# A decoder layer's second norm: four row tiles turned through VectorE and DRAM, gates reordered, and two buffers and chunk sizes changed

## Chip, cores and metric

The kernel runs on one core of one Trainium2 chip. The metric is the device time of one execution in microseconds (us); lower is better. TensorE is called PE, VectorE DVE, ScalarE ACT, GpSimd POOL and SyncE SP. Each is a queue that executes its instructions in order; DMAs are issued by SP, ACT and POOL.

## What is computed

One decoder layer on 1024 tokens and 16 meta tokens ahead of them (1040 rows), model width 1024, in float32. Two head groups share one input projection: sliding-window attention with sinks, and a gated linear recurrence (RG-LRU) behind a causal convolution. Their outputs are joined, projected, normed and added; then a feed-forward block with a squared ReLU is added in the same way.

```
u  = rmsnorm(h, g_pre_mix);  q, k, v, xr, yr = split(u @ w_in)
attn = sliding_window_attention_with_sinks(q, k, v, sinks)       # window 128
xr = causal_depthwise_conv(xr)
r = sigmoid(xr @ w_a + b_a);  i = sigmoid(xr @ w_x + b_x)        # in blocks of 64
a = exp(-8 r softplus(-lambda));  u = sqrt(1 - a^2) * i * xr
hr[t] = a[t] * hr[t-1] + u[t]
mix = concat(attn, gelu(yr) * hr) @ w_out
h = h + rmsnorm(mix, g_post_mix)
u = rmsnorm(h, g_pre_ffn);  f = square(relu(u @ w_ff1)) @ w_ff2
h = h + rmsnorm(f, g_post_ffn)
```

## The kernel before

**Precision.** Nearly every product is made of three matmuls (mm3, L123): each operand is split into a high part (a cast, usually on ACT, L96) and a low part (the rest, on DVE, L99); high x high, high x low and low x high are added in one bank of PSUM (the accumulator memory that PE writes). So a "split" of a tile costs one pass on ACT and one on DVE.

**Order of the work.** The program is written in one order and then put in order for each engine by a scheduler that plans with estimated costs; pieces can be marked as fill ("deferred", with FILL_LAG), so that PE does them where the main line has nothing ready. `behind(name, ins)` adds an order between two instructions (the scheduler must place the second after the first; no wait of its own at run time). Buffers come from pools by a tag: "raw" has 2 slots, "ws" 5, "a" 16, "b" 17, "c" 8, "d" 4 and "e" 2; PSUM banks carry the tags acc, s, pt and o, two of each. A new tile of a tag waits until the tile that last had its slot is no longer read.

**Stages, by the trace's times.**

1. To about 55 us: first norm, transposes, keys, values and the first queries.
2. To about 192 us: attention in eight steps (`scores`, `attend`, from L610 on), each step one pair of heads and one quarter of the rows. A step ends with a drain: ACT copies half of a bank, DVE adds the other half (L705, L706). Between the steps stand the fills: projections of two query groups, of four chunks of x (`fill_x`) and of four chunks of y (`fill_y`). `project` runs over eight slices of the model width and over the column pieces in a list; x uses ALL (272, 256, 256, 256 columns) and y REAL2 (two of 512). DVE copies each finished y piece out (L751).
3. 194 to 211 us: `gates(c)` for four chunks c of the recurrence (L805): three pieces of columns, two gates s, each on one half of PE's rows, three products: 18 matmuls of 64x348 a chunk into the banks s, pt and o in turn, and a sigmoid on ACT per bank (L824, through the helper at L82). Fill matmuls stand between the gates. The first of the sigmoids is preceded by a load of ACT's function table.
4. To about 260 us: `gather`, `decay` (exp and tanh on ACT), `recur` (square root on ACT; scale, product and scan on DVE: L850 to L852), gelu of y, `rec_out` (product with y and the split, L854), for chunks 0 and 1 and then 2 and 3. The output projection's weights are loaded and split among them (`load_wo`, `split_wo`; kc counts its eight slices). kc 0 to 3 take attention and need no recurrence; kc 4 and 5 need chunks 0 and 1, kc 6 and 7 chunks 2 and 3, by `rec_out`.
5. 226 to 332 us: `out_mm(t)` (L922), the output projection of eight tiles of 128 rows; tiles 0 to 3 first do kc 0 to 3, then 4 and 5, and the rest in the loop at L1113. `out_norm(t)` (L938): two reductions (rs, computed with POOL and DVE), scale by gmix_b (L951), residual (L954), a store of the row tile, and the second norm's scale (L959). `u2_tiles(t)` (L962) turns the normed tile with eight PE transposes (L971) and writes the result, times g_ffn_col, from PSUM into u2f: half by ACT (L982), half by DVE (L976). u2f[0] (tiles 0 to 3) and u2f[1] (tiles 4 to 7) are the halves of the feed-forward block's input.
6. To about 630 us: the first feed-forward product as a block scheme with seven instead of eight products. `operand` splits u2f tiles (b11 and b21 from u2f[0]); `t_sums` and `t_rest` form sums of the halves.
7. To the end (953 us): the second one: `steps` are 7 products (i) by 8 slices (q), 56 steps n = 8 i + q. `fetch_2(n)` loads one or two weight blocks into "raw" and "e" (L1261); for some q the second block is added to the first by a DMA of POOL (L1267). `prep_2(n)` splits the result.

Of the kernel before, what the change touches and what calls it, by code (L numbers as in the profile page):

```python
# [9 lines left out]
F32 = mybir.dt.float32  # L10
F32R = mybir.dt.float32r
AF = mybir.ActivationFunctionType
ALU = mybir.AluOpType
# [3 lines left out]
P = 128  # L17
D = 1024
# [19 lines left out]
def hybrid_layer(  # L38
# [248 lines left out]

    ALL = [(0, 272), (272, 256), (528, 256), (784, 256)]
    REAL2 = [(16, 512), (528, 512)]

# [318 lines left out]
    def scores(jp, quarter):  # L609
# [57 lines left out]
            )  # L667
        return sn

    def attend(jp, quarter, sn):  # L670
        flat = sn.rearrange("p a b c -> p (a b c)")
        pp = []
        for h in range(2):

            ph, pl = (slot("c", [P, 4, 2, P], F32R) for _ in range(2))
            pt = bank("pt")
            for i in range(4):
                nc.tensor.transpose(pt[:, i * P : (i + 1) * P], sn[:, h, i, 0:P], ident)
            pt = pt.rearrange("p (a b) -> p a b", a=4)
            split(ph[:, :, 0], pl[:, :, 0], pt)  # L680
            for p_ in (ph, pl):
                for s, g, op in ((1, 1, ALU.is_ge), (0, -1, ALU.is_gt)):
                    nc.gpsimd.affine_select(  # L683
                        out=p_[:, :, s], in_=f32(p_[:, :, 0]), pattern=[[0, 4], [g, P]],
                        compare_op=op, fill=0.0, base=0, channel_multiplier=-g,
                    )
            pp.append((ph, pl))
        kb0 = 2 * quarter
        for h in range(2):
            po = bank("o")  # L690
            two = po.rearrange("p (j c) -> p j c", j=2)
            for n, (oc, pc, w) in enumerate(((0, 0, P), (0, P, 2 * P), (P, 3 * P, P))):
                kb = kb0 + n
                v = vk[h][:, kb - 1, :] if kb else vm[:, h, :]
                for k, p_ in enumerate(pp[h]):
                    nc.tensor.matmul(  # L696
                        two[:, :, oc : oc + w], v,
                        p_.rearrange("p (j i) s c -> p j (i s c)", j=2)[:, :, pc : pc + w],
                        start=n == 0 and k == 0, stop=n == 2 and k == 1,
                        skip_group_check=True,  # L700
                    )

            r, o = HALF[h], HALF[1 - h]
            whole = flat[r, 0:512]
            nc.scalar.copy(whole, po[o, :])  # L705
            nc.vector.tensor_tensor(whole, po[r, :], whole, op=ALU.add)  # L706
        ah, al = at[quarter // 2][jp]
        c = slice(256 * (quarter % 2), 256 * (quarter % 2) + 256)
        split(
            ah[:, :, c], al[:, :, c],  # L710
            flat[:, 0:512].rearrange("p (j c) -> p j c", j=2),
        )
# [26 lines left out]
    def fill_x(c):  # L739
        def run(w):  # L740
            xr, sink = new_x()
            project(w, ALL, sink)
            conv(c, xr, "b" if c == 3 else "d")
        return run

# [59 lines left out]
    def gates(c):  # L805
        ch, cl = pair("b", [P, TT])
        split(ch, cl, xc[c])


        z = [slot("c", [P, TT]) for _ in range(2)]  # L810
        for t0, n in ((0, 348), (348, 348), (696, 344)):
            acc = []
            for s in range(2):
                flip[0] += 1
                acc.append(bank(("s", "pt", "o")[flip[0] % 3]))
            for k, (a, b) in enumerate(((0, ch), (0, cl), (1, ch))):
                for s in range(2):
                    nc.tensor.matmul(
                        acc[s][:, :n], gw[HALF[s], a, c, :], b[HALF[s], t0 : t0 + n],
                        start=k == 0, stop=k == 2, skip_group_check=True,  # L820
                    )
# [116 lines left out]
    def out_norm(t, po):  # L938
        xr = slot("d", [P, D])
        nc.sync.dma_start(xr, x[t * P : (t + 1) * P, :])  # L940
        h = slot("raw", [P, D])
        ssq = [small.tile([P, 1], F32, name=f"sq{n}", tag=f"sq{n}") for n in range(2)]
        for n in range(2):
            c = slice(512 * n, 512 * n + 512)
            nc.scalar.activation(
                h[:, c], po[n], AF.Square, scale=RMS_SC, accum_out=ssq[n]
            )
        rs = rstd_of(ssq)
        for n in range(2):
            c = slice(512 * n, 512 * n + 512)  # L950
            nc.vector.scalar_tensor_tensor(  # L951
                h[:, c], po[n], rs, gmix_b[:, c], op0=ALU.mult, op1=ALU.mult
            )
        nc.vector.tensor_tensor(h, h, xr, op=ALU.add)  # L954
# [4 lines left out]
        nc.vector.tensor_scalar(xr, h, rs2, None, op0=ALU.mult)  # L959
        return xr  # L960

# [34 lines left out]
    def combine(dst, x0, x1, op):  # L996
        return nc.vector.tensor_tensor(dst, x0, x1, op=op).ins  # L997

    def operand(tiles):
        pairs = []  # L1000
        for t_ in tiles:
            hi, lo = pair("b", [P, 2, 512])
            split(hi, lo, t_)
            pairs.append((hi, lo))
        return pairs

# [132 lines left out]
    def t_sums(c):  # L1139
        for i in range(2):  # L1140
            combine(t3[i][:, :, c], u2f[1][2 + i][:, :, c], u2f[1][i][:, :, c], ALU.subtract)
            combine(t2[i][:, :, c], t3[i][:, :, c], u2f[0][i][:, :, c], ALU.add)
            hi, lo = ot2[i]
            split(hi[:, :, c], lo[:, :, c], t2[i][:, :, c])

# [15 lines left out]
    def t_rest(k):  # L1161
        i = k % 2
        if k < 2:
            behind(mark[0], combine(u2f[1][i], u2f[1][i], u2f[0][i], ALU.subtract))
        elif k < 4:
            behind(mark[0], combine(t2[i], u2f[0][2 + i], t2[i], ALU.subtract))
        else:
            hl = pair("a", [P, 2, 512])
            late = mark[0]
# [340 lines left out]
```

## Time and profile before

| | |
|---|---|
| median of 3 runs | 956.37 us (955.89 to 956.82) |
| the profiled execution's own time | 954.71 us |
| its span in the trace | 953.0 us |
| granted TensorE clock in it | 0.999 |

A line of the profile gives a start or a count, the busy time, the engine, the line of the code (often that of a helper: L96, L98 and L99 are the split, L125, L130 and L131 the three products, L82 every table function of ACT, L997 `combine`), the operation, and "out<-in" by the names of tiles and tags, with partitions x elements and type; "x2" says that two instructions are shown as one. In brackets stands the idle time of the engine ahead of it and what ended that. In the list of waits a row says who waited, for whom, the microseconds in total, how often, and the longest. A DMA's row gives its number, size and the median time from issue to landing.

### The profile page before, as it was taken

How to read it: one execution, taken by the hardware profiler on the slowest of the kernel's cores; microseconds unless marked ns; L12 is line 12 of the kernel's file. 1: busy time of each engine (PE TensorE's matmuls, PEld its weight loads, DVE VectorE, ACT ScalarE, POOL GpSimd, SP SyncE). 2: the span in 40 equal slices, each digit the busy share in tenths (PEclk: the TensorE clock that was granted, in tenths of full speed). 3: DMA queues.
4: the chain of work that ended last, by engine and by line, in shares of the span. 5: the costliest groups of instructions: out<-in, count | busy, mean ns of one | idle time of the engine just before them, and what ended most of it. 6: DMA issues, size and time to landing. Idle time of an engine off the chain costs nothing.

```text
span 953.0 us, 12421 instructions
## 1 busy us (share of the span) xinstructions
PE 941.2 (99%) x4712; PEld 787.1 (83%) x4712; DVE 658.9 (69%) x849; ACT 507.8 (53%) x858; POOL 132.1 (14%) x205
## 2 busy tenths in 40 slices
PE   9999999999999999999999999999999999999997
PEld 8999999877888878888888888888888788888885
DVE  6668788879865887665644465476568576769883
ACT  8546766568645564443655575654433343445441
POOL 4104546410020100010000000001111100001201
PEclk9999999999999999999999999999999999999999
DMA  8220011104225468674422364334778765637934
GB/s 272 56 67 23 24 45 44 46 23 133 86 108 174 142 220 266 199 239 151 163 89 88 111 201 131 101 114 117 175 171 202 180 199 178 198 134 201 241 66 89
DMA packets 88199, 130.21 MB, mean 137 GB/s; under 512 B 13702, under 2 KB 52630, under 8 KB 88140
## 3 DMA queue, kind: packets, MB, share of 16 engines
q1 hardware_dynamic: 78972, 104.44, 34.4%
q0 software_dynamic: 8880, 24.19, 11.9%
q8 instruction: 37, 0.61, 0.3%
q10 hardware_dynamic: 288, 0.79, 0.2%
q14 instruction: 22, 0.18, 0.1%
HBM read 109.93 MB, written 18.87 MB: 135 GB/s over the span
## 4 chain that ended last, share of the span: by engine, by line
PE 91%; DVE 5%; ACT 2%; issue 1%; DMA 0%; DVEq 0%; SPq 0%
PE ps_acc L125 10%; PE ps_acc L131 10%; PE ps_acc L130 10%; PE ps_s L131 6%; PE ps_s L130 6%; PE ps_s L125 6%; PE ps_pt L130 6%; PE ps_pt L131 6%; PE ps_pt L125 6%; PE ps_o L131 5%; PE ps_o L130 5%; PE ps_o L125 5%; ACT c L82 1%; PE ps_o L696 1%; PE ps_acc L282 1%
## 5 line engine op out<-in xcount | busy, mean ns | idle before, releaser
L99 DVE TENSOR_TENSOR ws<-raw,ws 128x1024 fp32r<-128x1024 f32 (+1 forms) x69 | 82.6, 1197 | 71.0 <-ACT ws L96 24.1
L96 ACT CAST ws<-raw 128x1024 fp32r<-128x1024 f32 (+1 forms) x68 | 69.7, 1025 | 92.8 <-PE ps_o L130 25.0
L125 PE MATMUL ps_acc<-a,ws 128*128 128x256 f32 (+2 forms) x272 | 88.6, 326 | 0.7 <-DVE b L479 0.4
L130 PE MATMUL ps_acc<-a,ws 128*128 128x256 f32 (+2 forms) x272 | 87.9, 323 | 0.0
L96 ACT CAST ws<-e 128x1024 fp32r<-128x1024 f32 x41 | 43.0, 1050 | 83.4 <-PE ps_o L130 33.2
L131 PE MATMUL ps_acc<-a,ws 128*128 128x256 f32 (+2 forms) x272 | 87.5, 322 | 0.0
L99 DVE TENSOR_TENSOR b<-b,b 128x1024 fp32r<-128x1024 f32 (+2 forms) x50 | 58.9, 1178 | 24.7 <-PE ps_o L130 19.5
L99 DVE TENSOR_TENSOR ws<-e,ws 128x1024 fp32r<-128x1024 f32 x41 | 50.1, 1222 | 33.4 <-ACT ws L96 20.0
L96 ACT CAST b<-b 128x1024 fp32r<-128x1024 f32 (+2 forms) x49 | 50.0, 1019 | 43.6 <-DVE b L997 38.1
L683 POOL TENSOR_SCALAR_AFFINE_SELECT c<-c 128x512 fp32r<-128x512 f32 x64 | 55.5, 884 | 68.9 <-ACT c L96 54.9
L125 PEld LDWEIGHTS ps_acc<-a,ws 128*128 128x128 f32 x272 | 51.3, 188 | 5.4 <-issue 0.9
L131 PEld LDWEIGHTS ps_acc<-a,ws 128*128 128x128 f32 x272 | 51.2, 188 | 4.0 <-issue 0.2
L130 PEld LDWEIGHTS ps_acc<-a,ws 128*128 128x128 f32 x272 | 51.2, 188 | 3.7 <-issue 0.2
L125 PE MATMUL ps_acc<-ws,b 128*128 128x512 f32 (+1 forms) x120 | 46.4, 388 | 1.1 <-ACT ws L96 1.1
L130 PE MATMUL ps_acc<-ws,b 128*128 128x512 f32 (+1 forms) x120 | 46.2, 385 | 0.1
L131 PE MATMUL ps_acc<-ws,b 128*128 128x512 f32 (+1 forms) x120 | 46.2, 385 | 0.0
L125 PE MATMUL ps_pt<-ws,b 128*128 128x512 f32 x112 | 44.2, 395 | 0.0
L131 PE MATMUL ps_pt<-ws,b 128*128 128x512 f32 x112 | 44.1, 394 | 0.0
L130 PE MATMUL ps_pt<-ws,b 128*128 128x512 f32 x112 | 44.1, 393 | 0.0
L125 PE MATMUL ps_s<-ws,b 128*128 128x512 f32 x110 | 43.5, 395 | 0.0
L130 PE MATMUL ps_s<-ws,b 128*128 128x512 f32 x110 | 43.4, 394 | 0.0
L131 PE MATMUL ps_s<-ws,b 128*128 128x512 f32 x110 | 43.2, 393 | 0.0
(413 smaller groups left out, 2660.0 us busy)
## 6 DMA issues: line engine op xcount, KB each, us to landing
raw<-in_w_ff_dram SPq DMA_DIRECT2D x61, 512.0 KB, 3.5
e<-in_w_ff_dram SPq DMA_DIRECT2D x45, 512.0 KB, 4.0
a<-in_w_ff_dram SPq DMA_DIRECT2D x12, 512.0 KB, 5.5
s_dram<-a POOLq DMA_DIRECT2D x12, 512.0 KB, 3.8
raw<-in_w_in_dram SPq DMA_DIRECT2D x9, 512.0 KB, 3.8
c<-in_x_dram SPq DMA_DIRECT2D x8, 512.0 KB, 4.9
d<-in_x_dram SPq DMA_DIRECT2D x8, 512.0 KB, 4.6
out_dram<-raw SPq DMA_DIRECT2D x8, 512.0 KB
```

Of the source, the lines that this page charges most:

```text
L82: ins = nc.scalar.activation(*args, **kwargs).ins
L96: nc.scalar.copy(hi, src)
L99: low = nc.vector.tensor_tensor(lo, src, f32(hi), op=ALU.subtract).ins
L125: ins = nc.tensor.matmul(dst, lh, rh, start=start, stop=False, skip_group_check=True).ins
L130: nc.tensor.matmul(dst, lh, rl, start=False, stop=False, skip_group_check=True)
L131: last_mm[0] = nc.tensor.matmul(dst, ll, rh, start=False, stop=stop, skip_group_check=True).ins.name
L282: last_mm[0] = nc.tensor.matmul(acc[:, :n], w[k // 2][:, kc, :], u[kc][k % 2][:, t0 : t0 + n], start=k == 0 and kc == 0, stop=k == last an ...
L683: nc.gpsimd.affine_select(out=p_[:, :, s], in_=f32(p_[:, :, 0]), pattern=[[0, 4], [g, P]], compare_op=op, fill=0.0, base=0, channel_multip ...
L696: nc.tensor.matmul(two[:, :, oc : oc + w], v, p_.rearrange("p (j i) s c -> p j (i s c)", j=2)[:, :, pc : pc + w], start=n == 0 and k == 0, ...
```

## The change

Five edits in one diff.

- The list THIRDS replaces ALL for x (three pieces of 348, 348 and 344 columns instead of four) and names the gates' pieces, which were the same.
- `attend` remembers its last drain; the first product of both gates of chunk 0's first piece is ordered behind it.
- Tiles 0 to 3 of the second norm no longer go through `u2_tiles`. `u2_store` scales the row tile by rs and by the whole row of g_pre_ffn (a new broadcast tile in a slot of "ws") into an order in which a transpose of 32x32 blocks on DVE gives the wanted layout up to a regrouping of partitions; the result goes to DRAM from a tile of tag "e". `u2_read`, one tile later in the program, brings it back with four DMAs into u2f[0], which now has the shape 128 x 16 x 2 x 32. The sums and splits that read u2f[0] address it in runs of 32.
- The tiles that are still turned on PE come two tiles later in the loop over t: 4 and 5 ahead of the norm of tiles 6 and 7, 6 and 7 behind.
- `fetch_2` takes the second weight block of the products i = 1 and 2 from tag "d" instead of "raw" or "e".

```diff
+    THIRDS = [(0, 348), (348, 348), (696, 344)]
...
-            nc.vector.tensor_tensor(whole, po[r, :], whole, op=ALU.add)
+            drained[0] = nc.vector.tensor_tensor(
+                whole, po[r, :], whole, op=ALU.add
+            ).ins.name
...
-            project(w, ALL, sink)
+            project(w, THIRDS, sink)
...
+                    if c == 0 and t0 == 0 and k == 0:
+                        behind(drained[0], ins)
...
-    u2f = [[None] * 4 for _ in range(2)]
+    u2f = [[slot("c", [P, 16, 2, 32]) for _ in range(4)], [None] * 4]
+    u2_dram = dpool.tile([4, 4, P, 2 * P], F32, name="u2_dram")
+    gpre_b = slot("ws", [P, D])
+    nc.scalar.dma_start(gpre_b, g_pre_ffn[0].partition_broadcast(P))
+
+    def dealt(t_):
+        return t_.rearrange("p (k d b) -> p k d b", k=KC, b=4)
+
+    def u2_store(t, h, rs, tmp):
+        nc.vector.scalar_tensor_tensor(
+            tmp.rearrange("p (b k d) -> p k d b", b=4, k=KC), dealt(h), rs,
+            dealt(gpre_b), op0=ALU.mult, op1=ALU.mult,
+        )
+        y = slot("e", [P, D])
+        nc.vector.transpose(y, tmp)
+        nc.sync.dma_start(u2_dram[t].rearrange("a (d b) r -> (a d) (b r)", b=4), y)
+
+    def u2_read(t):
+        for q in range(4):
+            nc.sync.dma_start(
+                u2f[0][q][:, 4 * t : 4 * t + 4].rearrange("p a k t -> p a (k t)"),
+                u2_dram[t, :, :, 64 * q : 64 * q + 64].rearrange("a p r -> p a r"),
+            )
...
         rs2 = rstd_of([ssq2])
+        if t < 4:
+            u2_store(t, h, rs2, xr)
+            return None
         nc.vector.tensor_scalar(xr, h, rs2, None, op0=ALU.mult)
...
+    def rows(t_, c=slice(0, 512)):
+        if len(t_.shape) == 4:
+            return t_[:, c.start // 32 : c.stop // 32]
+        return t_[:, :, c].rearrange("p k (g t) -> p g k t", t=32)
...
-        for t_ in {4: (0,), 5: (2,), 6: (4,), 7: (5,)}.get(t, ()):
-            u2_tiles(t_, xns[t_])
+        if t > 5:
+            u2_tiles(t - 2, xns[t - 2])
         xns[t] = out_norm(t, po)
-        for t_ in {4: (1,), 5: (3,), 7: (6,)}.get(t, ()):
-            u2_tiles(t_, xns[t_])
+        if 1 <= t <= 4:
+            u2_read(t - 1)
+        if t == 7:
+            u2_tiles(6, xns[6])
...
         tags = (("raw", "e"), ("e", "raw"))[n % 2] if i < 6 else LASTW[q]
+        if i in (1, 2):
+            tags = tags[0], "d"
```

More of the change, by code (lines that the diff above doesn't have):

```diff
@@ L668, in scores @@
         return sn
+    drained = [None]
     def attend(jp, quarter, sn):
@@ L810, in gates @@
         z = [slot("c", [P, TT]) for _ in range(2)]
-        for t0, n in ((0, 348), (348, 348), (696, 344)):
+        for t0, n in THIRDS:
             acc = []
@@ L817, in gates @@
                 for s in range(2):
-                    nc.tensor.matmul(
+                    ins = nc.tensor.matmul(
                         acc[s][:, :n], gw[HALF[s], a, c, :], b[HALF[s], t0 : t0 + n],
                         start=k == 0, stop=k == 2, skip_group_check=True,
-                    )
+                    ).ins
+                    if c == 0 and t0 == 0 and k == 0:
+                        behind(drained[0], ins)
             for s in range(2):
@@ L1002, in operand @@
             hi, lo = pair("b", [P, 2, 512])
-            split(hi, lo, t_)
+            if len(t_.shape) == 4:
+                split(rows(hi), rows(lo), t_)
+            else:
+                split(hi, lo, t_)
             pairs.append((hi, lo))
@@ L1141, in t_sums @@
             combine(t3[i][:, :, c], u2f[1][2 + i][:, :, c], u2f[1][i][:, :, c], ALU.subtract)
-            combine(t2[i][:, :, c], t3[i][:, :, c], u2f[0][i][:, :, c], ALU.add)
+            combine(rows(t2[i], c), rows(t3[i], c), rows(u2f[0][i], c), ALU.add)
             hi, lo = ot2[i]
@@ L1163, in t_rest @@
         if k < 2:
-            behind(mark[0], combine(u2f[1][i], u2f[1][i], u2f[0][i], ALU.subtract))
+            behind(mark[0], combine(rows(u2f[1][i]), rows(u2f[1][i]), u2f[0][i], ALU.subtract))
         elif k < 4:
-            behind(mark[0], combine(t2[i], u2f[0][2 + i], t2[i], ALU.subtract))
+            behind(mark[0], combine(rows(t2[i]), u2f[0][2 + i], rows(t2[i]), ALU.subtract))
         else:
```

## The prediction

> **What bounds the kernel now.** I read the busy shares first, then the list of TensorE's own waits, then ten-microsecond windows.
>
> ```profile
> span 953.0 us, 12421 instructions
> PE 941.2 (99%) x4712; PEld 787.1 (83%) x4712; DVE 658.9 (69%) x849; ACT 507.8 (53%) x858; POOL 132.1 (14%) x205
> ```
> ```profile
> PE ps_acc L308 <- DVE base_e L562: 1.5, 1, 1.5
> PE ps_acc L125 <- ACT ws L96: 1.1, 1, 1.1
> ...
> PE ps_pt L130 <- DVE a L99: 0.2, 1, 0.2
> ```
>
> PE works for 99% of the span, and its seven waits (the first two and the last shown) add up to 4.6 us. So the time is PE's instructions plus those few waits: an edit gains only by taking matmuls off PE or by ending one of the waits, and loses only by making PE wait. Work moved to VectorE (DVE), ScalarE (ACT) or a queue costs nothing until PE runs out of work. The profiled execution's own time is 954.71 us (953.0 span and 1.7 around it). That is 1.66 below the median of 956.37. I sum against 954.71 and add the 1.66 at the end.
>
> **Step 1: tiles 0 to 3 are no longer turned on PE (a gain).**
>
> ```profile
> 281.10 1.03 PE L971 MATMUL ps_o<-ident,d 128*128 128x128 f32 x8
> 281.89 0.48 PE L125 MATMUL ps_acc<-ws,b 128*128 128x512 f32 x1
> 282.21 0.39 PE L130 MATMUL ps_acc<-ws,b 128*128 128x512 f32 x1
> ```
>
> From 281.10 to 282.21 PE spends 1.11 us on eight transposes and one matmul. A matmul alone takes 0.23 (step 2), so a tile's transposes cost 0.88. Four tiles: **-3.5 us**, as PE has no wait there.
>
> In exchange each of the four tiles gets, on DVE, a scaled copy that writes its row in another order, and a transpose of 32x32 blocks, in place of one multiply (L959). SP gets one 512 KB store and four reads of 128 KB in 256-byte runs.
>
> ```profile
> 263.48 1.41 DVE L951 SCALAR_TENSOR_TENSOR raw<-ps_pt,rs,e 128x512 f32<-128x512 f32 x2 [0.75 <-POOL rs L176]
> 264.93 1.23 DVE L954 TENSOR_TENSOR raw<-raw,d 128x1024 f32<-128x1024 f32 x1
> ...
> 268.34 0.75 DVE L959 TENSOR_SCALAR d<-raw,rs 128x1024 f32<-128x1024 f32 x1 [2.12 <-POOL rs L176]
> ```
> ```profile
> 248.99 4.53 DVE L852 TENSOR_TENSOR_SCAN c<-b,b 128x1040 f32<-128x1040 f32 x2
> ```
> ```profile
> s_dram<-a POOLq DMA_DIRECT2D x12, 512.0 KB, 3.8
> ...
> e<-s_dram SPq DMA_DIRECT2D x8, 512.0 KB, 3.2
> ```
>
> No row has either new operation. Lower ends: 0.75 for the transpose (L959), 1.23 for the copy (L954). Upper end for each: the scan, the slowest row per element, at 2.3. I take 1.25 for both, by L954, a plain pass over a tile of the same size. PE hands tiles 0 to 3 over within 11 us (12 matmuls each are left) and then takes 11 for every later tile (48 matmuls), so DVE works off a backlog, and the point to watch is tile 5, whose first matmul (281.89, before the transposes went 281.1) needs tile 2's banks. In the changed order DVE does, from 268.34: copy of tile 0, L951 of tile 1, transpose of tile 0, L954, the wait of 2.12, copy of tile 1, L951 of tile 2: 268.34 + 1.25 + 1.41 + 1.25 + 1.23 + 2.12 + 1.25 + 1.41 = 278.3. Cover 2.8; PE doesn't wait. At 2.3 for each new pass it would be 281.4, a wait of 0.3. Tiles 6 and 7 come 11 and 22 us later and DVE catches up. Then the turned rows: two more such rounds of 7.3 put the end of tile 3's transpose near 294; its store lands near 298 (3.8), the reads near 302 (3.2 by the row, more for the short runs), and the splits (passes of 1.2 like L954) end by 305 for b11 and 308 for b21. PE first multiplies b11 after tile 7, three tiles of 11 behind 281, near 314. Nine us of cover; cost 0.
>
> [...]
>
> **Step 2: x in three pieces (a small gain).**
>
> ```profile
> 72.38 0.28 PE L130 MATMUL ps_acc<-a,ws 128*128 128x256 f32 x1
> ...
> 76.04 0.28 PE L131 MATMUL ps_acc<-a,ws 128*128 128x256 f32 x1
> ```
> ```profile
> 258.87 0.39 PE L125 MATMUL ps_pt<-a,b 128*128 128x512 f32 x1
> ...
> 261.65 0.39 PE L125 MATMUL ps_o<-a,b 128*128 128x512 f32 x1
> ```
>
> Over 31 steps a 256-column matmul takes 3.66 / 31 = 0.118; over 12 steps one of 512 takes 2.78 / 12 = 0.232. Twice 0.118 less 0.232 is 0.004: the fixed part of a matmul. Four chunks x 8 slices x 3 products x 1 piece = 96 matmuls fewer at the same columns: **-0.4**. ACT's four evictions fewer lie beside PE. The scheduler orders the whole attention stage anew, where the list of waits shows under 1 us to win or lose by name; I take 0, within -1 to +2.
>
> **Step 3: the first gates held behind the last attention drain (a loss).** No wait is added, only an order. In the order of the changed kernel, PE does 4 fill matmuls after the last value product, then all gates of chunk 0, then at once those of chunk 1; before, fills stood between.
>
> ```profile
> 191.81 0.58 ACT L705 COPY c<-ps_o 64x512 f32<-64x512 f32 x1 [4.96 <-PE ps_o L696]
> 192.42 1.06 ACT L96 CAST b<-b 128x1040 fp32r<-128x1040 f32 x1
> ...
> 196.03 1.28 ACT L82 ACT_TABLE_LOAD   x1 [1.80 <-PE ps_pt L818]
> 197.33 0.55 ACT L82 ACTIVATE c<-ps_s,prm 128x348 f32<-128x348 f32 x1
> 197.78 0.55 ACT L82 ACTIVATE c<-ps_pt,prm 128x348 f32<-128x348 f32 x1
> ```
> ```profile
> 204.98 0.43 PE L818 MATMUL ps_s<-b,e 64*128 64x348 f32 x1
> 204.99 0.42 PE L818 MATMUL ps_pt<-b,e 64*128 64x348 f32 x1
> ...
> 206.61 0.50 PE L125 MATMUL ps_acc<-a,ws 128*128 128x512 f32 x1
> ```
>
> The gates of a chunk (18 matmuls, two halves of the array at once) take 1.63 us. Let T be the end of the last value product. Chunk 0's gates run from T + 1.0 to T + 2.6. ACT has the copy (to T + 0.6), two casts (to T + 2.2) and the table load (1.28): its first sigmoid runs T + 3.5 to 4.05, and the next two end 0.45 apart. Chunk 1's gates need those three banks, and PE's queue is in order: they start at T + 4.1, 4.55 and 5.0 and end at T + 5.7. Unhindered, they would end at T + 3.6. **+2.1**, between 1.3 (only the first bank waits) and 2.5. The runs also pair the halves less well: counting the longer half of each run, 42 steps instead of 39, at 0.16: **+0.5**.
>
> **Step 4: the recurrence behind it (a loss).** After the last gate the changed order leaves PE 38 fills before out_mm; before it had 63. So ACT's decays and DVE's scans start later against out_mm.
>
> ```profile
> 212.47 1.28 ACT L82 ACT_TABLE_LOAD   x1
> ...
> 234.36 1.28 ACT L82 ACT_TABLE_LOAD   x1
> ...
> 236.73 1.04 ACT L96 CAST a<-d 128x1024 fp32r<-128x1024 f32 x1
> ```
> ```profile
> 244.38 2.40 DVE L850 SCALAR_TENSOR_TENSOR c<-b,c 128x1040 f32<-128x1040 f32 x2 [1.27 <-ACT c L82]
> ...
> 256.43 0.69 DVE L99 TENSOR_TENSOR b<-d,b 128x512 fp32r<-128x512 f32 x1
> ```
> ```profile
> 225.83 0.39 PE L125 MATMUL ps_pt<-ws,b 128*128 128x512 f32 x1
> ```
>
> Before, out_mm runs unbroken from 225.83. ACT's two table loads for the decays stand 21.9 apart (212.47 and 234.36), and the second chunk pair's first two low halves, which kc 6 needs, are done 22.8 after the second (257.12). PE asks for them at 259.3 (two matmuls behind the one at 258.87, step 2): 2.2 to spare. After, call the start of out_mm 0. The 38 fills put the last gates at -8.8, and the first table load, behind their last sigmoids (two pitches of 0.45), at -7.9. With 21.9 the second stands at 14.0, with 22.8 the halves are ready at 36.8; two weight casts (236.73 is one) that stood in the second stretch now stand in the first, so up to 1.9 less. PE asks at 147 matmuls x 0.231 = 34.0. The wait is 0.9 to 2.8 by this; I take **+2.0**, with 0 to 4 for the range, as the first stretch holds loads that can land sooner or later. A wait for kc 5, whose low half now stands on DVE behind a scale that waits for the second square root, lies inside these 2.0. The present wait on L99 (0.2 in the list) goes: **-0.3** with the slow matmul after it.
>
> **Step 5: the second weight block of W2's steps i = 1, 2 gets buffer d (a gain).**
>
> ```profile
> 740.95 1.20 POOL L1267 DMA_DIRECT2D e<-in_w_ff_dram  x1 [7.62 <-DVE b L997]
> 748.76 1.22 POOL L1267 DMA_DIRECT2D raw<-in_w_ff_dram  x1 [6.61 <-issue]
> ```
> ```profile
> 754.82 1.04 ACT L96 CAST ws<-raw 128x1024 fp32r<-128x1024 f32 x1 [7.79 <-PE ps_o L131]
> ```
> ```profile
> 754.42 0.40 PE L131 MATMUL ps_o<-ws,b 128*128 128x512 f32 x1
> 755.91 0.50 PE L125 MATMUL ps_acc<-ws,b 128*128 128x512 f32 x1 [1.09 <-ACT ws L96]
> ...
> 756.72 0.40 PE L125 MATMUL ps_o<-ws,b 128*128 128x512 f32 x1
> 757.17 0.50 PE L130 MATMUL ps_acc<-ws,b 128*128 128x512 f32 x1
> ```
>
> The adding DMA of step 22 is issued at 748.76, behind that of step 23, and lands near 754.8; the cast, and PE, wait for it. PE's gaps beyond 0.23 from 754.42 to 757.7 (1.26, 0.22, two of 0.11) make 1.7. In the changed order step 22's base load no longer waits for the buffer of step 21, and its adding DMA comes first on POOL: about 7.8 earlier, landing near 743 to 747, for a need at 749 to 754. **-1.7**, between 0 and -1.7.
>
> **Sum:** -3.5 - 0.4 + 2.1 + 0.5 + 2.0 - 0.3 - 1.7 = -1.3. So 953.4 in the profiled execution, **955.1** by the median (a range of its own of 953 to 957.5).
>
> **Rivals.** (a) *The recurrence is hidden.* If the chain of step 4 ends before PE's need and the attention stage's new order wins a little, only step 3 is paid: -1.3 - 2.0 = -3.3, and 1 off: about **952**. For it speaks that DVE has gaps (1.27 before L850); against it that 25 fills of 0.23 are 5.8 us and only 2.2 were spare. (b) *The gains are undone by waits*: the reordered attention stage costs 2, or the recurrence its 4: -1.3 + 2 to 3, about **957.5**. (c) *Slower: the strided copy.* At L954's 1.23 it hides. Two copies lie ahead of the release of tile 2's banks, and the cover is 2.8: from 1.25 + 1.4 = 2.65 us a copy on PE waits, and each further microsecond counts twice. [...] (d) *W2's stall stays*, as POOL's queue, not the buffer, sets it: **957**. Its rows speak against that: POOL idled 6.6 ahead of the late issue.
>
> [...]
>
> **How the numbers follow.** The worked sum 0.40, (a) 0.27, (b) 0.13, (c) 0.13, (d) 0.07. A measurement of this kernel can tell about 0.2% (1.9 us) from no change, so faster means under 954.5 and slower over 958.3. Faster: all of (a) and a third of the sum, 0.40. Slower: (c), half of (b) and a little of the sum, 0.23. The rest, 0.37, is within. The range is 951 to 960: below lies an (a) in which the gate wait is hidden too, above a strided copy of 5 us.
>
> **What would show it.** Right: 32 rows of transposes gone between 281 and 307; a PE wait of 1 to 2 us on ACT's sigmoids right behind the gates of chunk 0; waits of PE on rec_out's halves at out_mm's kc 5 and 6; no wait near 755. Wrong: PE waiting in out_mm of tiles 5 to 7 on L951 (the copy is dear), PE waiting on b11's split (the round trip is late), or a wait near 755 at another step.

## The result and the profile after

| | before | after |
|---|---|---|
| median of 4 runs each | 956.60 us (955.89 to 956.93) | 961.80 us (961.36 to 962.53) |
| the profiled execution | 954.71 us | 961.36 us |
| granted clock in it | 0.999 | 0.992 |

The ratio is 1.0055, with a 95% interval of 1.0037 to 1.0073: the change costs about 5 us, against a forecast of a gain of 1.3 and a range that ended at 960. The profiled execution of before lies 1.9 below its median and that of after 0.4, so the two traces are 6.4 apart at the last matmul where the medians are 5.2 apart. First the busy shares and the clock on the page of after:

```profile
PE 942.9 (98%) x4584; PEld 787.1 (82%) x4584; DVE 663.9 (69%) x845; ACT 503.1 (52%) x838; POOL 133.8 (14%) x205
...
PEclk9999999999999979999999999999999999999999
```

There are 128 matmuls fewer, 32 transposes of step 1 and 96 pieces of x from step 2, and yet PE is busy 1.7 us longer. The 7 in the row of the clock, in the fifteenth of the forty slices, points to the reason: there PE ran at less than full speed. Next the list of PE's own waits in after (who waited, for whom, the total, how often, the longest):

```profile
PE ps_pt L131 <- DVE b L99: 2.1, 2, 1.2
PE ps_pt L125 <- ACT a L96: 1.8, 1, 1.8
...
PE ps_s L823 <- ACT c L82: 1.5, 1, 1.5
PE ps_pt L131 <- DVE a L99: 1.1, 1, 1.1
PE ps_acc L130 <- DVE b L99: 0.8, 1, 0.8
```

Two of these were forecast: L823 on ACT's sigmoids (step 3) and L131 on DVE's b, twice (step 4). The wait of 1.1 near 755 is gone (step 5). Three are new and not in the forecast: L125 on ACT's a, L131 on DVE's a and L130 on DVE's b. They stand together, 337 to 347 us into the span, in the first feed-forward product. To see what they cost I lined up the two traces matmul by matmul from the end. At 330 us, in the first feed-forward product, after is 0.6 us **ahead**. At 360 it is 7.4 behind, then 7.8 to 8.1 through the feed-forward block up to 754, and 6.4 at the end. So nearly the whole loss falls into 30 us, between 330 and 360. One ten-microsecond window of it, in the view by windows of before and then of after (the first two figures are its length and PE's busy time, with PE's instructions behind; the last three are the clock, the share of the DMA engines and GB/s):

```profile
340.00:350.00 10.00, 10.00 (x45) 7.88 (x43) 9.70 (x16) 6.12 (x11) 0.00 (x0) 1.00 0.45 151
```
```profile
340.00:350.00 10.00, 8.13 (x19) 5.70 (x19) 8.17 (x16) 6.58 (x11) 0.00 (x0) 0.53 0.65 212
```

After does 19 matmuls where before does 45, at a clock of 0.53. PE's timeline of after shows the two losses, waits and slow matmuls:

```profile
337.19 0.47 PE L131 MATMUL ps_s<-b,e 128*128 128x512 f32 x1
339.50 0.50 PE L125 MATMUL ps_pt<-b,a 128*128 128x512 f32 x1 [1.84 <-ACT a L96]
339.83 0.40 PE L130 MATMUL ps_pt<-b,a 128*128 128x512 f32 x1
341.35 0.80 PE L131 MATMUL ps_pt<-b,a 128*128 128x512 f32 x1 [1.11 <-DVE a L99]
341.94 0.63 PE L125 MATMUL ps_pt<-b,a 128*128 128x512 f32 x1
342.37 0.63 PE L130 MATMUL ps_pt<-b,a 128*128 128x512 f32 x1
...
345.78 0.63 PE L125 MATMUL ps_acc<-b,e 128*128 128x512 f32 x1
347.17 0.79 PE L130 MATMUL ps_acc<-b,e 128*128 128x512 f32 x1 [0.76 <-DVE b L99]
...
350.75 0.42 PE L125 MATMUL ps_acc<-b,e 128*128 128x512 f32 x1
```

- Waits. The gaps 337.19 to 339.50, 339.83 to 341.35 and 345.78 to 347.17 are 2.31, 1.52 and 1.39 where a step (from one matmul's start to the next one's) takes 0.23 (0.43 at the slow clock): 2.1 + 1.3 + 1.0 = **4.4 us**.
- Clock. From 341.35 to 350.75 the matmuls are 0.43 apart instead of 0.23: 9.4 less the last wait of 1.0 is 8.4 for 19 steps, which take 4.4 at full speed: **4.0 us**. The clock's own record in the trace says half speed for 10.24 us from 340.5 on.

Together 8.4; the two traces differ by 8.1 there, since before has some small gaps near 350 itself.

**Why the operand was late.** The wait on `a` is for the third slice of weights of the second product of the block scheme: SP loads it into a "raw" slot (L1026), ACT casts it (L96), DVE makes its low half (L99). Here is that chain, from the scale of the last row tile on. First VectorE's, SyncE's and ScalarE's timelines of before, one fence each:

```profile
274.01 0.75 DVE L959 TENSOR_SCALAR d<-raw,rs 128x1024 f32<-128x1024 f32 x1 [2.11 <-POOL rs L176]
...
320.91 1.41 DVE L951 SCALAR_TENSOR_TENSOR raw<-ps_pt,rs,e 128x512 f32<-128x512 f32 x2
...
326.33 0.75 DVE L959 TENSOR_SCALAR d<-raw,rs 128x1024 f32<-128x1024 f32 x1
...
336.87 1.22 DVE L99 TENSOR_TENSOR a<-raw,a 128x1024 fp32r<-128x1024 f32 x1
```
```profile
328.00 6.35 SPq L994 DMA_DIRECT2D raw<-in_w_ff_dram  x3
```
```profile
333.66 1.06 ACT L96 CAST a<-raw 128x1024 fp32r<-128x1024 f32 x1
```

And the same three of after:

```profile
271.50 2.08 DVE L936 SCALAR_TENSOR_TENSOR d<-raw,rs,ws 128x1024 f32<-128x1024 f32 x1 [2.12 <-POOL rs L176]
...
274.72 1.24 DVE L941 STREAM_TRANSPOSE e<-d 128x1024 f32<-128x1024 f32 x1
...
279.25 2.08 DVE L936 SCALAR_TENSOR_TENSOR d<-raw,rs,ws 128x1024 f32<-128x1024 f32 x1 [2.10 <-POOL rs L176]
...
326.42 1.41 DVE L980 SCALAR_TENSOR_TENSOR raw<-ps_pt,rs,e 128x512 f32<-128x512 f32 x2 [0.66 <-POOL rs L176]
...
332.93 0.75 DVE L991 TENSOR_SCALAR d<-raw,rs 128x1024 f32<-128x1024 f32 x1
...
340.08 1.22 DVE L99 TENSOR_TENSOR a<-raw,a 128x1024 fp32r<-128x1024 f32 x1
```
```profile
333.75 2.13 SPq L1026 DMA_DIRECT2D raw<-in_w_ff_dram  x3
```
```profile
338.40 1.04 ACT L96 CAST a<-raw 128x1024 fp32r<-128x1024 f32 x1 [1.17 <-DMA raw<-in_w_ff_dram]
```

Read down, each step of after is late by about as much as the one above it, and a little is made up: the last tile's scale by 5.5 (326.42 for 320.91), the second norm's scale by 6.6, the load by 5.8, the cast by 4.7, the low half by 3.2. The load is issued 0.07 us after the second norm's scale has ended (332.93 + 0.75), which is what a load that needs the slot of that tile looks like (in before it is 0.9). The low half starts without a gap behind other work of DVE's in both traces, so what it stands in is DVE's own queue. In before the low half is ready at 338.09 and PE takes it at 338.52, three steps behind its last product before (337.83): there was **0.4 us to spare**, and no list of waits shows a thing that is only just in time. Where it starts: one tile takes DVE 7.75 us in after (279.25 less 271.50), 5.67 in before (274.01 less 268.34). Tile 4's scale stands at 296.63 for 286.18, tile 5's at 307.62 for 295.72, tile 6's at 318.75 for 314.54. Not all of this is step 1's: 3.2 us are there at tile 0's scale already (266.64 for 263.48), behind the later gates and recurrence, which make PE late as well. What step 1 adds is seen against PE, whose last product for the last tile is this one, in before and then in after:

```profile
318.57 0.40 PE L131 MATMUL ps_pt<-a,b 128*128 128x512 f32 x1
```
```profile
317.94 0.40 PE L131 MATMUL ps_pt<-a,b 128*128 128x512 f32 x1
```

DVE's scale of that tile starts 2.3 us behind it in before (320.91) and 8.5 behind it in after (326.42).

### The profile page after: what moved, and what is told of

It reads as the page before. It is cut to its first block, busy times and chain, and to the rows that moved or that the text cites. A ratio compares the mean times of both kernels' runs of the same rounds, so it can differ in the third digit from the quotient of the medians.

```text
span 959.7 us, 12172 instructions
## 1 busy us (share of the span) xinstructions
PE 942.9 (98%) x4584; PEld 787.1 (82%) x4584; DVE 663.9 (69%) x845; ACT 503.1 (52%) x838; POOL 133.8 (14%) x205
## 4 chain that ended last, share of the span: by engine, by line
PE 85%; DVE 5%; ACT 3%; DMA 3%; issue 2%; POOL 1%; SPq 0%; DVEq 0%; ACTq 0%; POOLq 0%
PE ps_acc L130 11%; PE ps_acc L131 10%; PE ps_acc L125 10%; PE ps_s L131 5%; PE ps_s L125 5%; PE ps_s L130 5%; PE ps_pt L131 5%; PE ps_pt L125 5%; PE ps_pt L130 5%; PE ps_o L130 5%; PE ps_o L125 5%; PE ps_o L131 5%; PE ps_o L699 2%; PE ps_acc L282 1%; PE ps_s L629 1%
## 5 line engine op out<-in xcount | busy, mean ns | idle before, releaser
L99 DVE TENSOR_TENSOR ws<-raw,ws 128x1024 fp32r<-128x1024 f32 (+1 forms) x69 | 82.4, 1194 | 69.9 <-PE ps_o L130 23.1
L96 ACT CAST ws<-raw 128x1024 fp32r<-128x1024 f32 (+1 forms) x68 | 69.7, 1026 | 80.7 <-PE ps_o L130 33.6
L96 ACT CAST ws<-e 128x1024 fp32r<-128x1024 f32 x41 | 43.0, 1049 | 85.5 <-PE ps_o L130 38.1
L130 PE MATMUL ps_acc<-a,ws 128*128 128x512 f32 (+3 forms) x240 | 82.9, 346 | 0.0
L125 PE MATMUL ps_acc<-a,ws 128*128 128x512 f32 (+3 forms) x240 | 82.4, 344 | 0.0
L131 PE MATMUL ps_acc<-a,ws 128*128 128x512 f32 (+3 forms) x240 | 82.3, 343 | 0.0
L99 DVE TENSOR_TENSOR b<-b,b 128x1024 fp32r<-128x1024 f32 (+2 forms) x50 | 58.9, 1178 | 27.7 <-PE ps_o L130 22.5
L96 ACT CAST b<-b 128x1024 fp32r<-128x1024 f32 (+2 forms) x49 | 50.0, 1020 | 41.8 <-DVE b L1029 35.7
L99 DVE TENSOR_TENSOR ws<-e,ws 128x1024 fp32r<-128x1024 f32 x41 | 50.2, 1223 | 30.6 <-ACT ws L96 17.2
L130 PEld LDWEIGHTS ps_acc<-a,ws 128*128 128x128 f32 x240 | 45.1, 188 | 4.0 <-issue 0.6
L131 PEld LDWEIGHTS ps_acc<-a,ws 128*128 128x128 f32 x240 | 45.2, 188 | 3.8 <-issue 0.4
L125 PEld LDWEIGHTS ps_acc<-a,ws 128*128 128x128 f32 x240 | 45.1, 188 | 3.7 <-DVE b L99 0.2
L131 PE MATMUL ps_acc<-ws,b 128*128 128x512 f32 (+1 forms) x120 | 46.2, 385 | 0.0
L130 PE MATMUL ps_acc<-ws,b 128*128 128x512 f32 (+1 forms) x120 | 46.2, 385 | 0.0
L125 PE MATMUL ps_acc<-ws,b 128*128 128x512 f32 (+1 forms) x120 | 46.0, 385 | 0.0
L125 PE MATMUL ps_pt<-ws,b 128*128 128x512 f32 x112 | 44.2, 395 | 0.0
L131 PE MATMUL ps_pt<-ws,b 128*128 128x512 f32 x112 | 44.2, 394 | 0.0
L130 PE MATMUL ps_pt<-ws,b 128*128 128x512 f32 x112 | 44.1, 394 | 0.0
L130 PE MATMUL ps_s<-ws,b 128*128 128x512 f32 x110 | 43.4, 394 | 0.0
L131 PE MATMUL ps_s<-ws,b 128*128 128x512 f32 x110 | 43.3, 394 | 0.0
L125 PE MATMUL ps_s<-ws,b 128*128 128x512 f32 x110 | 43.3, 394 | 0.0
```

The source lines that it names most:

```text
L96: nc.scalar.copy(hi, src)
L99: low = nc.vector.tensor_tensor(lo, src, f32(hi), op=ALU.subtract).ins
L125: ins = nc.tensor.matmul(dst, lh, rh, start=start, stop=False, skip_group_check=True).ins
L130: nc.tensor.matmul(dst, lh, rl, start=False, stop=False, skip_group_check=True)
L131: last_mm[0] = nc.tensor.matmul(dst, ll, rh, start=False, stop=stop, skip_group_check=True).ins.name
```

## The experiments

The theory was that **step 1 fails by its cover**: turning four tiles on DVE puts the last tile's norm further behind PE, and with it the loads, casts and low halves that stand behind it in order, which had 0.4 us to spare. PE waits, and then runs at half clock. The rivals: the late gates and recurrence (steps 3 and 4) shift everything; the order of the "raw" buffers; the strided copy by itself; the x pieces. For each kernel I work out from its trace how long the low half of `a` was ready ahead of PE (its start plus its duration, against the start of PE's last product before it plus 0.69 for three steps):

| kernel | tiles turned on DVE | ready | PE could use it | to spare |
|---|---|---|---|---|
| before | 0 | 338.09 | 338.52 | 0.4 |
| after | 4 | 341.30 | 337.88 | -3.4 |
| e1_no_turn | 0 | 340.20 | 341.57 | 1.4 |
| e2_turn_only | 4 | 338.18 | 335.31 | -2.9 |
| e3_no_hold | 4 | 337.56 | 334.13 | -3.4 |
| e5_all_pieces | 4 | 341.83 | 337.50 | -4.3 |
| e6_plain | 4 | 341.36 | 339.64 | -1.7 |
| e8_other_buffer | 4 | 345.46 | 340.09 | -5.4 |
| e9_low_on_pool | 4 | 343.76 | 335.49 | -8.3 |
| e10_two_tiles | 2 | 336.10 | 336.26 | 0.2 |
| e11_pieces_w2 | 0 | 342.04 | 342.91 | 0.9 |

The same traces show how far DVE is behind PE, from PE's last product for tile 7 to that tile's scale: 2.3 us in before, 2.0 in e1_no_turn and e11_pieces_w2, 3.0 in e10_two_tiles, and with four tiles turned 6.8 (e2_turn_only, e6_plain) to 8.5 (after, e8_other_buffer) and 12.3 (e9_low_on_pool). In all of them the low half starts on DVE without a gap. The column "ready" by itself can mislead: in e2_turn_only the low half is ready at 338.18, as in before (338.09). It is PE that gets there 3.2 earlier, since it no longer turns those tiles, and DVE's queue does not come earlier with it.

The median of before differs between the chips used (955.36, 956.86 and 957.36 us), so each kernel is given as a ratio to it.

### e1_no_turn: after, without step 1

Tiles 0 to 3 go through `u2_tiles` on PE again; the sums in `t_rest` add the columns of these four tiles in another order than the reference, at the same cost: such a sum of 128x1024 takes DVE 1.22 us in the plain order (before) and 1.22 in this one (after).

```diff
-    u2f = [[slot("c", [P, 16, 2, 32]) for _ in range(4)], [None] * 4]
...
+    u2f = [[None] * 4 for _ in range(2)]
...
-        if t < 4:
-            u2_store(t, h, rs2, xr)
-            return None
```

> The changed kernel with tiles 0 to 3 turned on PE again; the other edits stay. Backlog theory (the two dearer passes on DVE in out_norm make the row buffers, and so the early weights, late; PE waits 3.7 us near 337 to 347 and its clock then halves for 10 us): no wait and full clock there, so 956.6 - 0.4 (x pieces) + 1.6 (gates) + 2.4 (recurrence) - 0.3 - 1.7 (W2) = 958.2. Late-start rival (the gates and the recurrence, which come later, make the norm late): PE still waits near 337 and the clock still halves, 962 to 966.

Measured: 956.89 us, ratio 1.0014 (1.0001 to 1.0027). No wait and no slow clock near 337 (1.00 from 340 to 350). The waits of steps 3 and 4 stand as in after (1.5 on L82; 2.0 on L99 in two waits). So 0.4% of the 0.55% comes with step 1, and steps 3 and 4 alone don't make the wait at 337.

### e2_turn_only: before, with step 1 alone

Relative to after, the hold (the order of step 3), the pieces of x and the buffer of W2 are undone:

```diff
-            project(w, THIRDS, sink)
+            project(w, ALL, sink)
...
-                    if c == 0 and t0 == 0 and k == 0:
-                        behind(drained[0], ins)
...
-        if i in (1, 2):
-            tags = tags[0], "d"
```

> The kernel before with the turning of tiles 0 to 3 through DVE and DRAM alone. Backlog theory: -3.5 for the transposes, and the waits and half clock near 335 to 350 as in the changed kernel, +8: 961. Late-start rival: the norm starts as early as before, no wait, full clock: 953.1. Queue rival (SP's stores and reads stand ahead of the weight loads; DVE's passes don't matter): 961 as well.

Measured: 960.23 us, ratio 1.0057 (1.0038 to 1.0076): one of the five edits loses as much as the five together. PE's timeline of this kernel has the same picture:

```profile
334.62 0.40 PE L131 MATMUL ps_s<-b,e 128*128 128x512 f32 x1
335.75 0.50 PE L125 MATMUL ps_pt<-b,a 128*128 128x512 f32 x1 [0.73 <-ACT a L96]
...
338.24 0.79 PE L131 MATMUL ps_pt<-b,a 128*128 128x512 f32 x1 [1.77 <-DVE a L99]
338.83 0.63 PE L125 MATMUL ps_pt<-b,a 128*128 128x512 f32 x1
```

Lined up with before, this kernel is 3.3 ahead where the block scheme begins, 2.2 behind at 360 and 4.1 behind at 400, after one more wait of 1.2 on ACT's e at 364. (Near 755 it waits 1.8 where before waits 1.1, so a little of its loss lies outside step 1's place.) The gain of step 1 is therefore real (forecast: 3.5) and more than given back in the place that has no cover. With gates and recurrence as in before, the rival of the late start is not needed for this wait.

### e4_w2_only: before, with step 5 alone

```diff
+        if i in (1, 2):
+            tags = tags[0], "d"
```

> The kernel before with the other buffer in W2's steps alone. If step 5 is right, the wait near 755 goes and nothing else moves: 954.9. If POOL's queue set that wait: 956.6.

Measured: 953.33 us, ratio 0.9981 (0.9967 to 0.9995). The wait of L125 on ACT's ws is gone, and the two traces differ by 1.7 us, all of it near 755. Step 5 holds, size and place.

### e6_plain: after, with the copy in plain order

The reordering is left out, so the turned rows land in other places.

```diff
-            tmp.rearrange("p (b k d) -> p k d b", b=4, k=KC), dealt(h), rs,
-            dealt(gpre_b), op0=ALU.mult, op1=ALU.mult,
+            tmp, h, rs, gpre_b, op0=ALU.mult, op1=ALU.mult,
```

> The changed kernel with the scaled copy written in plain order, without the 1 KB stride (so the turned rows land in wrong places: the reordering is left out). Backlog theory: the copy falls from 2.08 to about 1.25 us, the early weights come about 3 us earlier, PE waits under 1 us and keeps its clock: 954 to 956. Queue rival: the SP queue is the same, so 961 to 962.

Measured: 957.19 us, ratio 1.0023 (1.0012 to 1.0034): 0.3% is regained, less than expected. VectorE's timeline has the plain copy:

```profile
273.26 1.28 DVE L936 SCALAR_TENSOR_TENSOR d<-raw,rs,ws 128x1024 f32<-128x1024 f32 x1 [2.12 <-POOL rs L176]
```

The stride therefore costs 0.80 a copy (2.08 less 1.28), 3.2 for four. Without it the low half is still 1.7 late, and PE waits 1.5 on it. The strided copy is a part of the cause and not the whole. In this profile the half clock at 337 is gone (1.00 from 340 to 350), but one of 3.41 us stands behind the gates at 203; its execution is the slowest of the seven (959.00). So the 0.3% is the shorter wait and the missing half clock together.

### e7_fill: after, with work for PE in the wait

Twelve matmuls whose result is overwritten stand ahead of the second product of the block scheme:

```diff
+        if p == 2:
+            for _ in range(12):
+                nc.tensor.matmul(
+                    y2, a12_early[1][0][:, 0, :], b21[0][0][:, 0, :], start=True,
+                    stop=True, skip_group_check=True,
+                )
```

> The changed kernel with twelve matmuls of 128x512 more, right ahead of p2(2), into the bank that p2(2) then starts anew; the result doesn't change. They lie in PE's wait of 1.84 and 1.11 us near 337 to 341 and delay nothing by more than 0.3. If the half clock there comes from PE standing still, it stays away: 961.8 - 4 = 958, with a clock of 0.998. If the half clock has another cause (heat or power after the dense stage before), it stays: 962.

Measured: 958.67 us, ratio 1.0031 (1.0016 to 1.0046), 0.24% below after. PE's timeline of this kernel:

```profile
337.70 3.03 PE L1152 MATMUL ps_pt<-b,ws 128*128 128x512 f32 x12 [0.25 <-DVE d L1157]
340.58 0.39 PE L125 MATMUL ps_pt<-b,a 128*128 128x512 f32 x1
...
341.17 0.50 PE L131 MATMUL ps_pt<-b,a 128*128 128x512 f32 x1
```

The low half comes hardly earlier (341.12 for 341.30); the fill takes the place of the wait. But behind it the matmuls are at full speed (0.39 where after has 0.63). So here the half clock came with PE's wait and stayed away where the wait was filled (a granted clock of 1.00 from 340 to 350, for 0.53 in after). What the fill regains, 0.24%, is 2.3 us; expected were 4.

### e8_other_buffer: after, with another slot for one earlier load

```diff
-            a11_early.update(early(0, 2, hl))
+            a11_early.update(early(0, 2, hl, "ws"))
```

(`early` takes the tag as an argument.)

> The changed kernel with the early weight block for p1(2) and p1(3) landing in a free slot of tag ws instead of raw; DVE's passes and SP's order stay. Buffer-chain theory (the two raw slots pass from row tile to weight block to row tile 7 to the weight block of p2(2), each behind the one before): that load is issued near 311 instead of 316.9, tile 7's norm starts 5 us earlier, p2(2)'s weights are there in time, the clock stays full: 954 to 956. Pure DVE theory (DVE's backlog itself sets when p2(2)'s weights are split): 961 to 962.

Measured: 960.51 us, ratio 1.0042 (1.0025 to 1.0060), and the low half later still (5.4). The earlier load goes out sooner (313.98 for 316.92), but the last tile's scale is at 328.68 and not before 326.42. Some 2.2 of the delays in this profile come from a spell of half clock at 203; its execution is the slowest of the six (962.93). Behind PE the last tile's scale stands at 8.5 us, as in after: on DVE tile 6's scale now stands behind the low halves of the block scheme, at 322.43 for 318.75. So this version of the theory, that the delay is handed on from one raw buffer to the next, fell. What is left is the order of DVE's and ACT's queues, in which norms and splits alternate; that is argued from the traces and no run changes that order alone.

### e3_no_hold: after, without steps 3 and 4

```diff
-                    if c == 0 and t0 == 0 and k == 0:
-                        behind(drained[0], ins)
```

> The changed kernel without the order that holds the first gates. If the hold makes the gate wait (1.6 us near 200), it goes, and the recurrence is no longer late by 2.3: 961.8 - 1.6 to 3.9 = 958 to 960. If the new order of the attention stage by the x pieces makes it, 961.8 stays.

Measured: 956.33 us, ratio 0.9993 (0.9979 to 1.0006), 0.62% below after. Neither the gates' nor the recurrence's wait is there; the low half is 3.4 late as before. Lined up with before, the kernel is 4.5 ahead at 330 and 0.6 behind at 360: step 1 alone takes 5.0 back here. In most executions it may well be more: the profiled one is the fastest of its ten (954.24), and its granted clock of 0.997 the highest (0.994 to 0.996 in the others). So steps 3 and 4 are a loss of their own, one that adds to that of step 1.

### e5_all_pieces: after, with x in four pieces

```diff
-            project(w, THIRDS, sink)
+            project(w, ALL, sink)
```

> The changed kernel with x in four pieces again, the hold kept. If the x pieces' new order of the attention stage is what brings the gates and the recurrence late (waits of 1.6 and 2.3), both go: 961.8 - 3.5 = 958. If the hold does it: 961.8 + 0.4 = 962.2.

Measured: 960.42 us, ratio 1.0042 (1.0027 to 1.0056). The waits at 337 (2.2 and 1.3) and 6.83 us of half clock stay. The pieces of x are not the cause. Their own worth can't be told, since other waits change with them: the gates' wait on L82 is gone here although the hold is kept, and the recurrence has smaller ones (0.4 at 215, 0.5 and 1.0 at 260). So the hold makes the gates' wait only together with the order that the three pieces bring.

### e9_low_on_pool: no hold, and two low halves moved from DVE to POOL

```diff
-                split(rows(hi), rows(lo), t_)
+                if low_on_pool:
+                    nc.scalar.copy(rows(hi), t_)
+                    nc.gpsimd.tensor_tensor(
+                        rows(lo), t_, rows(f32(hi)), op=ALU.subtract
+                    )
+                else:
+                    split(rows(hi), rows(lo), t_)
```

> The changed kernel without the hold, and with the two low halves of b21 made by POOL instead of DVE (2.4 us of DVE between tile 5 and tile 7). DVE-backlog theory: DVE's later work comes up to 2.4 earlier, PE's wait of 3.1 at p2(2) falls to about 1 and the clock stays full: against 956.3 without the hold alone, 951.5 to 953.5. Transfer rival (the weight block's load is late by itself): 956.

Measured: 962.05 us, ratio 1.0062 (1.0043 to 1.0082): a miss. POOL's and DVE's timelines of this kernel show why:

```profile
309.47 5.23 POOL L1041 TENSOR_TENSOR b<-c,b 128x1024 fp32r<-128x1024 f32 x2
```
```profile
309.53 2.89 DVE L989 TENSOR_SCALAR d<-raw,rs 128x1024 f32<-128x1024 f32 x1 [0.76 <-POOL rs L176]
312.34 3.44 DVE L99 TENSOR_TENSOR ws<-raw,ws 128x1024 fp32r<-128x1024 f32 x1
```

While POOL made the two halves, DVE's passes took 2.89 and 3.44 us where the same ones take 0.75 and 1.22 elsewhere. DVE lost 4.4 to save 2.4. The wait at 337 then grew to 4.8 and 2.6. More delay on DVE, more wait on PE: by its sign the miss speaks for the theory.

### e10_two_tiles: no hold, and only tiles 0 and 1 turned on DVE

```diff
-        if t < 4:
+        if t < 2:
...
-        if 1 <= t <= 4:
+        if 1 <= t <= 2:
             u2_read(t - 1)
+        if t in (4, 5):
+            u2_tiles(t - 2, xns[t - 2])
```

> The changed kernel without the hold, and with only tiles 0 and 1 through DVE and DRAM; tiles 2 and 3 on PE again. DVE-backlog theory: the added passes are 5 us instead of 10 and are worked off before tile 4; no wait at p2(2), full clock: 956.6 - 1.8 - 0.4 - 1.7 = 952.7. If the backlog isn't it (the later place of the PE turns, or the round trip): 955 to 957.

Measured: **951.35 us, ratio 0.9942 (0.9926 to 0.9957)**, faster than both kernels, and 0.5% faster than e3_no_hold, from which it differs by two tiles. PE's whole list of waits, and its timeline where the block scheme's second product starts:

```profile
PE ps_acc L309 <- DVE base_e L563: 1.5, 1, 1.5
PE ps_o L358 <- DVE d L248: 0.5, 1, 0.5
PE ps_s L358 <- DVE d L248: 0.2, 1, 0.2
```
```profile
335.57 0.39 PE L131 MATMUL ps_s<-b,e 128*128 128x512 f32 x1
335.80 0.39 PE L125 MATMUL ps_pt<-b,a 128*128 128x512 f32 x1
```

VectorE's timeline of the same kernel has the last tile's scale 7.1 us earlier than in after, and the low half 5.2 earlier:

```profile
319.28 1.41 DVE L978 SCALAR_TENSOR_TENSOR raw<-ps_pt,rs,e 128x512 f32<-128x512 f32 x2
...
334.88 1.22 DVE L99 TENSOR_TENSOR a<-raw,a 128x1024 fp32r<-128x1024 f32 x1
```

No wait is left behind the first 10 us. At 2.08 a tile (7.75 less 5.67) DVE has 4.2 us more to do than in before, where four tiles give it 8.3. The run halves the trips through DRAM along with this work, and it makes PE later: of the 3.6 us of slack that it has over e3_no_hold, 2.1 come from PE, which turns two tiles more, and 1.5 from the low half. So it shows that two trips through DRAM bring no wait and that half of the load fits, but it does not measure DVE's part alone.

### e11_pieces_w2: before, with the pieces of x and the buffer of W2

```diff
-        if t < 4:
-            u2_store(t, h, rs2, xr)
-            return None
...
-                    if c == 0 and t0 == 0 and k == 0:
-                        behind(drained[0], ins)
```

(The rest of step 1 is undone as in e1_no_turn.)

> The kernel before with the x pieces and the other buffer in W2, without hold and turning. The parts add up: 956.6 - 0.4 - 1.7 = 954.5, no wait near 200, 250, 337 and 755.

Measured: 958.19 us, ratio 1.0014 (1.0000 to 1.0027): a miss. It has waits of the recurrence that neither e3_no_hold nor e10_two_tiles has, in PE's list:

```profile
PE ps_pt L125 <- ACT b L96: 1.4, 1, 1.4
PE ps_pt L131 <- DVE b L99: 1.3, 2, 1.0
```

They stand at 259 to 263 us, with 3.41 us of half clock behind them. The edits do not add: the scheduler orders the recurrence anew with each of them, and without the hold and without step 1 it comes out worse. Why, I did not settle.

### e12_no_hold_fill: e3_no_hold, with the twelve matmuls of e7_fill

```diff
-                    if c == 0 and t0 == 0 and k == 0:
-                        behind(drained[0], ins)
...
+        if p == 2:
+            for _ in range(12):
...
```

> The changed kernel without the hold, with the twelve matmuls ahead of p2(2) that overwrite nothing. The half clock goes as it did with the hold: 956.3 - 2 to 4 = 952.5 to 954.5, clock 0.998. If the wait without the hold is too short for the fill, it costs up to 1: 957.

Measured: 955.22 us, ratio 0.9996 (0.9979 to 1.0013), not to be told from e3_no_hold. The half clock at 338 is gone and the wait down to 0.3, but the twelve matmuls cost 2.8 themselves, and a spell stands at 11 us in its profile: so the time decides nothing. The granted clock agrees with e7_fill: its median over ten executions is 0.998, for 0.995 in e3_no_hold.

## Why the prediction was wrong

**Step 1 failed, and with it the sign.** Its gain came: 3.3 us in e2_turn_only. What failed is the sentence "Tiles 6 and 7 come 11 and 22 us later and DVE catches up", and the cost of 0 that followed. It went wrong in three ways.

- *The price.* The transpose was right (1.25 taken, 1.24 measured); the copy was taken at 1.25 and is 2.08. The point from which rival (c) was to decide, 2.65, isn't reached, and tile 5's banks cause no wait, as the step said. The upper end of the range, 960, stood for a copy of 5 us, and no run shows one; against the plain copy's 1.28 in e6_plain the 2.08 is a factor of 1.6. With the plain copy 0.3 of the 0.55% is gone, the half clock included.
- *The cover.* DVE did not catch up with PE. Against before's times it nearly did: of the 10.4 us at tile 4, 5.5 were left at tile 7, of which 3.2 came with the late start, and in e2_turn_only, without that start, 1.2 were left (322.12 for 320.91). But by step 1's own gain PE is 3.3 us ahead there, and its operands had to come that much earlier. The step counted PE's distance to the turned rows (the nine microseconds of b11, which held: PE starts on b11 without a wait, though the reads, in runs of 256 bytes, took 4.0 us to land, for the 3.2 of the step's row), and not what else stands behind tile 7 in DVE's and ACT's queues: the weights of the next product. Their 0.4 us of slack was never looked up. In e10_two_tiles, with half of the work, the low half is 0.2 early.
- *The price of a wait.* 4.4 us of waits cost 8.4, as PE's clock was at half for 10.24 us from the second of them on. No term of the sum had that.

What stays open is the scheduler's share: each edit also changes the order of DVE's and ACT's queues, and no run held that order fixed.

**Step 2** stays unmeasured: -0.4 is too small to be told apart from the reordering in e5_all_pieces and e11_pieces_w2. The range of -1 to +2 that it gave for the reordering was too narrow: e11_pieces_w2 is 4.3 us behind before at 330, with the half clock behind its waits.

**Step 3** was right in kind and a little large: PE's gates of chunk 1 wait for ACT's sigmoids, in after's timeline,

```profile
199.40 0.32 PE L823 MATMUL ps_o<-b,e 64*128 64x344 f32 x1
201.20 0.73 PE L823 MATMUL ps_s<-b,e 64*128 64x348 f32 x3 [1.48 <-ACT c L82]
```

1.80 less a step of 0.23 is 1.6, where 2.1 was forecast (1.3 to 2.5). **Step 4** was right and a little small, at both of the named places, kc 5 and kc 6:

```profile
249.57 0.40 PE L131 MATMUL ps_pt<-a,b 128*128 128x512 f32 x1
251.18 0.50 PE L131 MATMUL ps_pt<-a,b 128*128 128x512 f32 x1 [1.22 <-DVE b L99]
...
260.80 0.39 PE L130 MATMUL ps_pt<-a,b 128*128 128x512 f32 x1
262.08 0.50 PE L131 MATMUL ps_pt<-a,b 128*128 128x512 f32 x1 [0.89 <-DVE b L99]
```

1.4 and 1.05 lost make 2.4 for 2.0. In e3_no_hold, without the hold, both waits vanish, and 0.62% with them; but the hold is not their only condition, as e5_all_pieces (hold kept, no wait at the gates) and e11_pieces_w2 (no hold, waits in the recurrence) show. **Step 5** was right, -1.7.

Up to 330 us the sum of steps 1 to 4 was thus nearly right: +0.4 was forecast (-3.5 - 0.4 + 2.1 + 0.5 + 2.0 - 0.3), -0.6 measured. Then come the 8.1 us that no step had, and the -1.7 of step 5. Of the rivals, (c) named the right part of the change and the wrong place; (a) and (d) fell, and (b) came closest in kind, waits that undo the gains, but with its waits in the wrong stage.

## What to carry to other kernels

Work that is moved to an engine with idle time is free only up to the next thing that this engine owes the critical one. And when a change makes the bottleneck engine faster, everything that feeds it has to come earlier by as much. Look for the operand that arrives last before the bottleneck engine needs it, work out its slack from the two timelines, and compare the added time with that slack, since a list of waits shows nothing that is just in time. Where a move costs more than the slack, do half of it: two tiles of four kept the gain here.

## What the runs showed of the hardware

- **Half clock after waits much shorter than the spell.** PE's granted clock fell to half in spells of 3.41 us (e6_plain, e11_pieces_w2), 6.83 (e5_all_pieces) and 10.24 (after), multiples of 3.41. In after no single idle stretch ahead of it was over 2.1 us: between 337.4 and 341.35 PE did two matmuls. The same wait of 1.5 at the gates was followed by a spell in e6_plain and e8_other_buffer and by none in after, e1_no_turn and e7_fill. So in these runs the length of one wait did not decide whether a spell followed; the exact condition stays open.
- **DVE's passes were slow beside POOL's.** POOL's subtraction of 128x1024 took 2.6 us a pass, and DVE's passes beside it, 2.89 and 3.44 us, took 3.9 and 2.8 times as long as the same ones elsewhere, 0.75 and 1.22 (e9_low_on_pool).
- **A write with 1 KB between neighbours** took 2.08 us for 128x1024 elements (after) where the plain one took 1.28 (e6_plain); a transpose of 32x32 blocks of the same tile took 1.24, no more than a plain pass (1.23, L954 in before).
